# Seven block products for eight in the down projection and the embeddings' gate of a hybrid encoder

## The chip, the cores and the metric

The kernel runs on one core of one Trainium2 chip. The metric is the device time of one execution in microseconds (us). The engines are named as in the profile: PE is TensorE's matmul and PEld its weight load, DVE is VectorE, ACT is ScalarE, POOL is GpSimd and SP is SyncE, which here only issues DMAs.

## The reference

One layer of an encoder works on x of 2048 rows by 1024 columns, all in float32:

```python
h = layer_norm(x, emb_ln_g, emb_ln_b)
z = h @ w_in                                     # 1024 x 1536
y_ssm = s5_mixer(z[..., :512], ...)              # diagonal state space, GELU, GLU
y_sgu = sgu_mixer(z[..., 512:], ...)             # gated unit, blocks of 128 rows
mix = concatenate([rms_norm(y_ssm), rms_norm(y_sgu)]) @ w_out
h = layer_norm(ALPHA * h + mix, ln1_g, ln1_b)
ffn = (silu(h @ w_ffn_gate) * (h @ w_ffn_up)) @ w_ffn_down    # 1024 -> 2816 -> 1024
ple = (p @ w_ple) * sigmoid(h @ w_ple_gate + b_ple_gate)      # p: 2048 x 256
out = layer_norm(ALPHA * h + ffn + ple, ln2_g, ln2_b)
```

## The kernel before

A product in the precision that is wanted takes three passes: each operand is split into a rounded part `hi` (a copy on ACT, line 63) and the rest `lo` (a subtraction on DVE, line 64), and `mm3` (lines 68 to 70) adds hi·hi, hi·lo and lo·hi in one bank of PSUM. A pass is one matmul of a 128x128 stationary block against 512 columns. `load_w` (line 262) loads weights through SP into one of three `raw` tiles of 128x1024, and the split halves stand in six `wsp` tiles. PSUM is eight banks, all from `bank()`. Instructions are emitted in program order with a priority. A scheduler lays them out on each engine in advance, so an engine takes them in a fixed order and waits in it.

`run` has three parts. The first makes `z` and the gated unit. The second is the state space part: for every four of the 32 groups `s5_coeffs` makes coefficient matrices (`CA1`, `BA`, `yrep` and `dg` on POOL, `CA2` on DVE), `s5_matrices` turns them on PE, and for each group `s5_in` runs the scan on DVE (lines 803 to 811) and `s5_out` the output products. Then `glu` and `out_proj`. The third is `phase_b`: `mixed` finishes `out_proj`, normalizes, writes the rows to `xnd` and their transposes to `hfd` in device memory, and two blocks of 1024 rows go through the rest.

For a block, `heads` and `others` load the transposes and split them, `sums_B` makes on POOL the four sums of the right hand operand (lines 1219 to 1222), which Winograd's form of seven products needs, and `ple` does the embeddings: for each half of the rows and of the columns, 4 row tiles by 8 k by three passes with `w_ple_gate`, then the bias and the sigmoid (lines 1123 and 1124), `p @ w_ple`, and the product of both into `acc`. Then 11 rounds (`i`) follow, each with 256 of the 2816 inner columns: `gate` and `up` go through `quarters`, seven products of 4 k by three passes, with sums of the weights on POOL in `ops_A` (lines 1234 to 1241, tile `S`). `up` multiplies and splits the result into four `ff` tiles. `down` of the round before stands between them: for 16 tiles of 128x512, two k by three passes, and DVE adds each bank to `acc` (line 1319). `residual` adds ALPHA·h in four steps a round, on POOL, with `rx` tiles loaded from `xnd` (lines 1141 to 1150). At the block's end `norm_out` normalizes the eight `acc` tiles (line 135 and 136 on DVE, 1167 on ACT, 1168 and 1169 on POOL) and stores them.

Of the kernel before, what the change touches and what calls it, by code (L numbers as in the profile page):

```python
# [13 lines left out]
P = 128  # L14
S = 2048
# [7 lines left out]
FF = 2816  # L23
ALPHA = 2.0 ** 0.25
# [25 lines left out]
class Kern:  # L50
# [100 lines left out]
    def run(self):  # L151
        nc, tc = self.nc, self.tc
        with ExitStack() as ctx:
# [17 lines left out]
            self.xnd = dt([S, D], F32, name="xnd")  # L171
            with ExitStack() as c1:
# [530 lines left out]
    def s5_setup(self, ctx):  # L703
# [5 lines left out]
        nc.gpsimd.memset(self.yrep, 0.0)  # L709
        for i in range(2):  # L710
# [7 lines left out]
    def s5_coeffs(self, q):  # L718

        nc, pl = self.nc, self.pl  # L720
        v, g = nc.vector, nc.gpsimd
# [9 lines left out]
        ar8 = self.akr[:, gs, 1:9].unsqueeze(3).broadcast_to(sh8)  # L731
        ai8 = self.aki[:, gs, 1:9].unsqueeze(3).broadcast_to(sh8)
# [4 lines left out]
        g.tensor_tensor(out=ca, in0=X1.broadcast_to(sh9), in1=ar9, op=ALU.mult)  # L737
        g.tensor_tensor(out=tA, in0=X2.broadcast_to(sh9), in1=ai9, op=ALU.mult)
        g.tensor_tensor(out=ca, in0=ca, in1=tA, op=ALU.add)
        CA2 = pl.tile(sh8, F32, name="CA2", tag="CA2", bufs=2)  # L740
        tB = pl.tile(sh8, F32, name="tB", tag="tB", bufs=1)
        v.tensor_tensor(out=CA2, in0=X2.broadcast_to(sh8), in1=ar8, op=ALU.mult)
        v.tensor_tensor(out=tB, in0=X1.broadcast_to(sh8), in1=ai8, op=ALU.mult)
        v.tensor_tensor(out=CA2, in0=CA2, in1=tB, op=ALU.subtract)
        BA = pl.tile(sh8, F32, name="BA", tag="BA", bufs=1)
        tC = pl.tile(sh8, F32, name="tC", tag="tC", bufs=1)
        g.tensor_tensor(out=BA, in0=Y1.broadcast_to(sh8), in1=rr8, op=ALU.mult)
        g.tensor_tensor(out=tC, in0=Y2.broadcast_to(sh8), in1=ri8, op=ALU.mult)
        g.tensor_tensor(out=BA, in0=BA, in1=tC, op=ALU.add)
        shq = [P, NQ, L // 2, HG]  # L750
        for par in range(2):
            yv = yrep[:, :, par].rearrange("p g (s two) h -> p g s two h", two=2)
            g.tensor_copy(out=yv[:, :, :, par, :], in_=Y1.broadcast_to(shq))
        self.dg = pl.tile([P, NQ, P], F32, name="dg", tag="tC", bufs=1)
        g.tensor_tensor(out=self.dg, in0=self.ident.unsqueeze(1).broadcast_to([P, NQ, P]),
                        in1=self.dvec[:, gs].unsqueeze(2).broadcast_to([P, NQ, P]), op=ALU.mult)
        self.mats[q] = (T, CA1, CA2, BA)

    def s5_matrices(self, q):
        nc, pl = self.nc, self.pl  # L760
        v, yrep = nc.vector, self.yrep
        T, CA1, CA2, BA = self.mats[q]
# [200 lines left out]
    def phase_b(self, ctx):  # L963
# [6 lines left out]
        for _ in range(3):  # L970
            next(mixed)
        B = self.heads(0)
        next(mixed)
        for blk in range(2):
# [3 lines left out]
            if blk == 0:  # L978
                for _ in mixed:
                    pass  # L980
# [369 lines left out]
```

## Time and profile before

| | |
|---|---|
| time of three runs | 2375.39 to 2377.78 us, median 2377.55 us |
| the profiled execution's own time | 2384.52 us |
| its span, first to last instruction | 2382.5 us |
| its mean granted TensorE clock | 0.973 |
| matmuls | 9876 |
| moved by DMA | 257.27 MB, mean 108 GB/s |

The page gives busy time for each engine over the span. A matmul is recorded with 0.39 us, though the next one begins 0.227 us after it: they overlap, and a PE that is busy all the time need not be doing all it can. What a matmul costs is therefore read from the starts. Two windows matter besides the busy shares: the waits (who waited for whom) and the chain of work that ended last. In the second and third quarter of the span the same pattern repeats every 60.5 us, one round of the inner loop.

### The profile page before, as it was taken

Reading aid. Unit: us, or ns where it says so; the run is one execution under the profiler, and the core shown is the slowest. Engines: PE = TensorE matmul, PEld = TensorE weight load, DVE = VectorE, ACT = ScalarE, POOL = GpSimd, SP = SyncE. Lnnn points to the kernel's source line nnn. Section 1 sums busy time; section 2 is a strip of 40 time slices with the busy share of each in tenths; the row PEclk is TensorE's granted clock in tenths of the full one; section 3 lists DMA queues with packets and bytes.
Section 4 is the critical chain, followed back from the end, with each engine's and each line's share of the span. In section 5 each row is a group of like instructions: output and inputs, shape, how many; then the busy total and the mean of one; then the engine's idle time right before and its main releaser. Section 6 shows DMA issues by size and latency. Waiting matters only on the chain.

```text
span 2382.5 us, 27557 instructions
## 1 busy us (share of the span) xinstructions
PE 2228.3 (94%) x9876; PEld 1826.3 (77%) x9876; DVE 1551.4 (65%) x2726; ACT 761.5 (32%) x1291; POOL 794.7 (33%) x775
## 2 busy tenths in 40 slices
PE   7899987898999989999999999969899999999994
PEld 6678876676788878888887878758788888878883
DVE  7996769968645555555655555775556555555558
ACT  4444432243323432222222222323422222222221
POOL 1188145300000244444334342123344444443214
PEclk9999999899999999999999999979999999999997
DMA  8547434446654522212212121354122222221112
GB/s 268 140 151 230 133 102 135 133 116 235 233 208 166 171 84 62 65 56 66 62 58 70 57 64 54 124 181 160 49 62 67 62 67 63 65 64 57 50 40 88
DMA packets 248700, 257.27 MB, mean 108 GB/s; under 512 B 55106, under 2 KB 183154, under 8 KB 248564
## 3 DMA queue, kind: packets, MB, share of 16 engines
q1 hardware_dynamic: 219572, 230.33, 30.7%
q10 hardware_dynamic: 27904, 20.98, 2.8%
q0 software_dynamic: 1088, 4.21, 0.5%
q8 instruction: 77, 1.26, 0.2%
q14 instruction: 59, 0.48, 0.1%
HBM read 200.93 MB, written 54.54 MB: 107 GB/s over the span
## 4 chain that ended last, share of the span: by engine, by line
PE 53%; POOL 7%; DVE 6%; issue 3%; ACT 3%; DMA 2%; POOLq 0%; ACTq 0%; SPq 0%; DVEq 0%
PE ps L68 18%; PE ps L70 17%; PE ps L69 17%; POOL tx L1294 3%; DMA tx<-hfd 2%; ACT ff L63 1%; DVE wsp L64 1%; DVE t L1274 1%; ACT wsp L63 1%; DVE t L1277 1%; DVE tx L1294 1%; PE ps L142 1%; DVE t L1270 1%; DVE acc L136 1%; POOL rx L1148 0%
## 5 line engine op out<-in xcount | busy, mean ns | idle before, releaser
L63 ACT CAST wsp<-raw 128x512 fp32r<-128x512 f32 x448 | 275.5, 622 | 790.7 <-PE ps L70 716.8
L64 DVE TENSOR_TENSOR wsp<-raw,wsp 128x512 fp32r<-128x512 f32 x438 | 342.6, 788 | 252.9 <-ACT wsp L63 250.5
L1319 DVE TENSOR_TENSOR acc<-acc,ps 128x512 f32<-128x512 f32 x352 | 240.6, 685 | 144.2 <-PE ps L70 143.3
L68 PE MATMUL ps<-wsp,ff 128*128 128x512 f32 x768 | 299.7, 390 | 4.1 <-ACT ff L63 4.1
L70 PE MATMUL ps<-wsp,ff 128*128 128x512 f32 x768 | 299.6, 390 | 0.0
L69 PE MATMUL ps<-wsp,ff 128*128 128x512 f32 x768 | 299.5, 390 | 0.0
L68 PE MATMUL ps<-hT,wsp 128*128 128x512 f32 x744 | 290.4, 391 | 5.7 <-ACT hT L308 5.7
L69 PE MATMUL ps<-hT,wsp 128*128 128x512 f32 x744 | 290.4, 391 | 1.0 <-DVE hT L309 1.0
L70 PE MATMUL ps<-hT,wsp 128*128 128x512 f32 x744 | 289.9, 390 | 0.0
L68 PE MATMUL ps<-hTx,wsp 128*128 128x512 f32 x616 | 244.4, 397 | 25.0 <-DVE t L1123 13.4
L70 PE MATMUL ps<-hTx,wsp 128*128 128x512 f32 x616 | 241.3, 392 | 0.0
L69 PE MATMUL ps<-hTx,wsp 128*128 128x512 f32 x616 | 241.3, 392 | 0.0
L1234 POOL TENSOR_TENSOR S<-raw 128x512 f32<-128x512 f32 x44 | 58.7, 1333 | 438.3 <-DMA raw<-in_w_ffn_up_dram 318.4
L68 PEld LDWEIGHTS ps<-wsp,ff 128*128 128x128 f32 x768 | 144.4, 188 | 34.9 <-ACT ff L63 4.9
L70 PEld LDWEIGHTS ps<-wsp,ff 128*128 128x128 f32 x768 | 144.6, 188 | 30.5 <-DVE ff L64 0.5
L69 PEld LDWEIGHTS ps<-wsp,ff 128*128 128x128 f32 x768 | 144.6, 188 | 29.9
L68 PEld LDWEIGHTS ps<-hT,wsp 128*128 128x128 f32 x744 | 140.3, 189 | 34.9 <-ACT hT L308 6.1
L69 PEld LDWEIGHTS ps<-hT,wsp 128*128 128x128 f32 x744 | 140.0, 188 | 31.0 <-DVE hT L309 2.2
L70 PEld LDWEIGHTS ps<-hT,wsp 128*128 128x128 f32 x744 | 140.1, 188 | 29.1
L68 PEld LDWEIGHTS ps<-hTx,wsp 128*128 128x128 f32 x616 | 116.5, 189 | 58.7 <-ACT tx L1259 19.9
L64 DVE TENSOR_TENSOR ff<-tx,ff 128x512 fp32r<-128x512 f32 x96 | 67.1, 699 | 119.6 <-ACT ff L63 119.4
L69 PE MATMUL ps<-wsp,hT 128*128 128x512 f32 x352 | 138.6, 394 | 4.7 <-DVE wsp L64 4.7
(314 smaller groups left out, 4241.6 us busy)
## 6 DMA issues: line engine op xcount, KB each, us to landing
raw<-in_w_in_dram SPq DMA_DIRECT2D x48, 512.0 KB
raw<-in_w_ffn_gate_dram SPq DMA_DIRECT2D x44, 512.0 KB
raw<-in_w_ffn_up_dram SPq DMA_DIRECT2D x44, 512.0 KB
raw<-in_w_ffn_down_dram SPq DMA_DIRECT2D x44, 512.0 KB
tx<-hfd SPq DMA_DIRECT2D x64, 256.0 KB
raw<-in_w_ple_gate_dram SPq DMA_DIRECT2D x32, 512.0 KB
CS<-tbd SPq DMA_DIRECT2D x64, 128.5 KB
xt<-in_x_dram SPq DMA_DIRECT2D x16, 512.0 KB
```

What stands on the lines that cost most here:

```text
L63: nc.scalar.copy(out=hi, in_=src)
L64: (e or nc.vector).tensor_tensor(out=lo, in0=src, in1=hi.bitcast(F32), op=ALU.subtract)
L68: mm(ps, lhsT=lh, rhs=rh, start=start, stop=False, skip_group_check=more)
L69: mm(ps, lhsT=lh, rhs=rl, start=False, stop=False, skip_group_check=more)
L70: mm(ps, lhsT=ll, rhs=rh, start=False, stop=stop, skip_group_check=more)
L136: nc.vector.scalar_tensor_tensor(out=dst, in0=dst, scalar=rstd, in1=b, op0=ALU.mult, op1=ALU.add)
L142: self.nc.tensor.transpose(ps[:, t * P:(t + 1) * P], x[:, col:col + P], self.ident)
L1234: g.tensor_tensor(out=s1, in0=a21, in1=a22, op=ALU.add)
L1270: v.tensor_tensor(out=y, in0=y, in1=d, op=ALU.add)
L1274: v.tensor_tensor(out=z, in0=x, in1=c, op=ALU.add)
L1294: e.tensor_tensor(out=f[n], in0=f[n], in1=q, op=ALU.mult)
L1319: v.tensor_tensor(out=xs, in0=xs, in1=ps, op=ALU.add)
```

## The change

`down` leaves the rounds. `up` no longer splits its result: it multiplies all four quarters on DVE, makes the sums that the seven products need from the left operand (four on DVE), and stores seven tiles of 128x512 a round to device memory (`fod`), through ACT's queue. In the first block `down_sums` loads `w_ffn_down` in every round, makes four sums of it on POOL and stores them (`wtd`). After the 11 rounds the new `down` runs seven block products. Each goes over 11 steps: load a left and a right tile of 128x512 (256 KB each, two DMAs into one `raw` tile), split both, four row tiles by three passes. `seven` holds two sets of four banks, so that sums of products form in PSUM, and reads each set once a product (four additions on DVE a product, where 16 a round stood). `residual` runs beside products 0 to 3 with tiles of 128x512; the next block's operands and sums are made between the products (`operands(1)`); `norm_out` of a block's first half is issued after product 5, the rest between the products of the next block's `ple`. The last product of the last block loads all its operands first and then finishes one row tile after another.

`ple` does the gate for both halves of the rows as seven products of 4 k, with weight sums made on POOL in `gate_sums` during `mixed` and stored to `pgd`. The bias comes in by PE (a matmul of 33 rows, as `mixed` does), 12 for a block.

In the state space part `CA1` and `BA` move from POOL to DVE, `CA2` becomes one matmul of `CA1` with a signed permutation (float32, 512 columns, one for four groups) and a copy on ACT, `yrep` and `dg` move to ACT. `tx` gets six buffers for four.

```diff
+    def seven(self, product, read):
+        u = [self.bank() for _ in range(4)]
+        product(0, u, True)
+        read(0, u)
+        yield
+        for n in range(1, 7):
+            if n % 2:
+                if n < 5:
+                    q = [self.bank() for _ in range(4)]
+                product(n, q, n < 5)
+                read(n, q)
+            else:
+                product(n, u, False)
+                read(n, u)
+            yield
...
     def phase_b(self, ctx):
...
+            for i in range(NP):
+                f = self.gate(w_g, i, self.B)
+                if blk == 0:
+                    self.down_sums(i)
+                self.up(blk, w_u, i, self.B, f)
+            B = self.operands(1) if blk == 0 else iter(())
+            tail = self.norm_out(blk, accs)
+            for _ in self.down(blk, accs, tail):
+                next(B, None)
...
+    def gate_sums(self, kks):
...
+        for kk in kks:
+            rA, rB = (self.load_w(W[kk][:, :, i * 512:(i + 1) * 512], 1024) for i in range(2))
...
+            g.tensor_tensor(out=a22, in0=a21, in1=a22, op=ALU.add)
+            g.tensor_tensor(out=a21, in0=a11, in1=a21, op=ALU.subtract)
+            g.tensor_tensor(out=a11, in0=a22, in1=a11, op=ALU.subtract)
+            g.tensor_tensor(out=a12, in0=a12, in1=a11, op=ALU.subtract)
+            self.nc.sync.dma_start(out=self.pgd[kk, 0], in_=rA)
+            self.nc.sync.dma_start(out=self.pgd[kk, 1], in_=rB)
...
     def ple(...):
+        def product(n, ps, start):
+            src, b = ops[n]
+            for k in range(4):
+                if k % 2 == 0:
+                    w = self.load_split(src(k), 1024)
+                h = self.B[b][k]
...
+                for t in range(4):
+                    self.mm3(ps[t], h[:, 0, t * P:(t + 1) * P], h[:, 1, t * P:(t + 1) * P],
+                             w[:, 0, ws], w[:, 1, ws], start and k == 0, k == 3, not start)
...
     def residual(self, blk, accs):
+        for tg in range(2):
+            for hf in range(2):
...
+                gb = self.pb.tile([P, 2, 512], F32, name="S", tag="S", bufs=1)
...
                 for t in range(4):
+                    x = self.txt()
...
     def up(...):
-            e = nc.vector if n in (0, 3) else nc.gpsimd
-            e.tensor_tensor(out=f[n], in0=f[n], in1=q, op=ALU.mult)
-            h = self.fft()
-            self.split(h[:, 0], h[:, 1], f[n])
...
+            v.tensor_tensor(out=f[n], in0=f[n], in1=q, op=ALU.mult)
...
+        store(0, a11)
+        store(6, a22)
+        v.tensor_tensor(out=s1, in0=a21, in1=a22, op=ALU.add)
+        store(3, s1)
+        v.tensor_tensor(out=s2, in0=s1, in1=a11, op=ALU.subtract)
...
     def down(...):
-            for ii in range(2):
-                ft = fts[ii][tg]
-                self.mm3(ps, ft[:, 0, t * P:(t + 1) * P], ft[:, 1, t * P:(t + 1) * P],
-                         w[hf][ii][:, 0], w[hf][ii][:, 1], ii == 0, ii == 1)
-            xs = accs[tg][t][:, cs]
-            v.tensor_tensor(out=xs, in0=xs, in1=ps, op=ALU.add)
+        def operands(n, i, kept):
+            r = self.rawt()
+            nc.sync.dma_start(out=r[:, :512], in_=self.fod[blk, i, n])
+            nc.sync.dma_start(out=r[:, 512:], in_=w[n](i))
+            out = []
+            for ii in range(2):
+                if kept:
+                    t = self.hTt() if 2 * i + ii < 14 else self.hxt()
+                else:
+                    t = self.wspt() if ii else self.fft()
+                self.split(t[:, 0], t[:, 1], r[:, ii * 512:(ii + 1) * 512])
+                out.append(t)
+            return out
...
+        def product(n, ps, start):
+            if n == 6 and blk:
+                ops = [operands(n, i, True) for i in range(NP)]
+                for t in range(4):
+                    for i in range(NP):
+                        passes(ps, t, i, ops[i], start)
+                return
+            for i in range(NP):
+                ops = operands(n, i, False)
+                for t in range(4):
+                    passes(ps, t, i, ops, start)
...
+        for n, _ in enumerate(self.seven(product, read)):
+            if n < 4:
+                next(rest)
+            if n == 5:
+                next(tail)
+                next(tail)
+            yield
...
     def s5_matrices(self, q):
+        psC = self.bank()
+        nc.tensor.matmul(psC, lhsT=self.swap, rhs=CA1[:, :, 2:10, :].rearrange("p g s h -> p g (s h)"),
+                         start=True, stop=True)
+        CA2 = pl.tile([P, NQ, L, HG], F32, name="CA2", tag="CA2", bufs=2)
+        nc.scalar.copy(out=CA2.rearrange("p g s h -> p (g s h)"), in_=psC)
```

## Rows read from the trace of the kernel before

**Rows 1.** The page, part 1: busy us, share of the span, instructions.

```profile
PE 2228.3 (94%) x9876; PEld 1826.3 (77%) x9876; DVE 1551.4 (65%) x2726; ACT 761.5 (32%) x1291; POOL 794.7 (33%) x775
```

**Rows 2.** Stretch, inner loop: busy PE, PEld, DVE, ACT, POOL; clock, DMA share, GB/s.

```profile
1800.00:1860.00 60.00, 59.67 (x264) 49.06 (x263) 35.97 (x50) 16.27 (x28) 26.29 (x24) 1.00 0.20 63
```

**Rows 3.** Timeline of PE: start, us; `down`'s first matmul and the first behind it.

```profile
1801.45 0.39 PE L68 MATMUL ps<-wsp,ff 128*128 128x512 f32 x1
...
1823.21 0.39 PE L68 MATMUL ps<-hTx,wsp 128*128 128x512 f32 x1
```

**Rows 4.** The chain that ended last: start, us; one step of two successive rounds.

```profile
958.23 0.70 DVE t L1270
...
1018.72 0.70 DVE t L1270
```

**Rows 5.** The same chain, out_proj: four bias matmuls.

```profile
641.43 1.13 PE ps L1030 x4
```

**Rows 6.** Waits of PE, 1500 to 1700 us: total us, times, longest.

```profile
PE ps L69 <- DVE wsp L64: 23.4, 1, 23.4
PE ps L68 <- DVE t L1123: 6.4, 1, 6.4
```

**Rows 7.** Waits of PE, 640 to 870 us.

```profile
PE ps L68 <- DVE t L1123: 7.0, 1, 7.0
```

**Rows 8.** Stretches between the blocks and at the second loop's start, columns as rows 2.

```profile
1550.00:1560.00 10.00, 0.00 (x0) 0.00 (x0) 10.00 (x19) 1.02 (x1) 9.92 (x4) 0.50 0.26 104
...
1680.00:1690.00 10.00, 9.26 (x31) 7.52 (x32) 8.99 (x15) 7.12 (x13) 1.96 (x2) 0.71 0.21 59
```

**Rows 9.** Timeline of DVE, 1500 to 1560 us: `norm_out` between the blocks.

```profile
1552.84 2.87 DVE L136 SCALAR_TENSOR_TENSOR acc<-acc,rs,ff 128x1024 f32<-128x1024 f32 x1
```

**Rows 10.** Stretch at the end, columns as rows 2.

```profile
2350.00:2360.00 10.00, 1.86 (x9) 1.21 (x7) 9.96 (x42) 1.99 (x3) 9.84 (x5) 0.74 0.14 56
```

**Rows 11.** The chain that ended last: its last step.

```profile
2377.57 1.28 DVE acc L136
```

**Rows 12.** Stretch in the state space part, columns as rows 2.

```profile
400.00:420.00 20.00, 16.74 (x75) 13.21 (x74) 19.92 (x31) 6.78 (x15) 11.67 (x11) 0.84 0.53 165
```

**Rows 13.** Groups, 300 to 490 us: count, busy us, mean ns, idle before.

```profile
L811 DVE TENSOR_TENSOR PQ<-Sx,CS 128x512 f32<-128x512 f32 x32 | 30.8, 962 | 0.3
...
L739 POOL TENSOR_TENSOR ca<-ca,tA 128x576 f32<-128x576 f32 x7 | 11.1, 1590 | 0.5
```

**Rows 14.** Groups over the span: `glu`'s four products in plain float32.

```profile
L884 PE MATMUL ps<-vs,ones 128*128 128x512 f32 x8 | 4.1, 592 | 0.0
```

**Rows 15.** Timeline of DVE, inner loop: a split alone, one beside POOL.

```profile
1814.15 0.68 DVE L64 TENSOR_TENSOR wsp<-S,wsp 128x512 fp32r<-128x512 f32 x1
...
1829.51 1.63 DVE L64 TENSOR_TENSOR wsp<-raw,wsp 128x512 fp32r<-128x512 f32 x1 [1.32 <-ACT wsp L63]
```

**Rows 16.** Timeline of POOL, inner loop: a step of `residual`, a sum of `ops_A`.

```profile
1815.39 0.74 POOL L1147 TENSOR_TENSOR rx<-rx,rg 128x256 f32<-128x256 f32 x1
...
1829.31 1.29 POOL L1239 TENSOR_TENSOR raw<-raw 128x512 f32<-128x512 f32 x1
```

**Rows 17.** The page, part 5: groups of instructions on DVE.

```profile
L64 DVE TENSOR_TENSOR wsp<-raw,wsp 128x512 fp32r<-128x512 f32 x438 | 342.6, 788 | 252.9 <-ACT wsp L63 250.5
L1319 DVE TENSOR_TENSOR acc<-acc,ps 128x512 f32<-128x512 f32 x352 | 240.6, 685 | 144.2 <-PE ps L70 143.3
```

**Rows 18.** Timeline of SP, out_proj: four loads of `w_out`, 512 KB each.

```profile
590.30 8.99 SPq L262 DMA_DIRECT2D raw<-in_w_out_dram  x4
```

**Rows 19.** Timeline of ACT: casts of the first and the last of these four.

```profile
594.69 1.14 ACT L63 CAST hTx<-raw 128x512 fp32r<-128x512 f32 x2 [0.96 <-DMA raw<-in_w_out_dram]
...
602.70 1.15 ACT L63 CAST ff<-raw 128x512 fp32r<-128x512 f32 x2 [2.17 <-DMA raw<-in_w_out_dram]
```

**Rows 20.** Stretch around these loads, columns as rows 2.

```profile
580.00:600.00 20.00, 20.00 (x88) 16.01 (x87) 17.64 (x32) 7.26 (x13) 1.92 (x1) 1.00 0.69 219
```

More of the change, by code (lines that the diff above doesn't have):

```diff
@@ L23 @@
 FF = 2816
+NP = FF // (2 * P)
 ALPHA = 2.0 ** 0.25
@@ new lines, in down_sums @@
+    def down_sums(self, i):
+        g = self.nc.gpsimd
+        w_d = self.a["w_ffn_down"][0].rearrange("(k p) c -> p k c", p=P)
+        rA, rB = (self.load_w(w_d[:, 2 * i + ii, :], 1024) for ii in range(2))
+        b11, b12, b21, b22 = rA[:, :512], rA[:, 512:], rB[:, :512], rB[:, 512:]
+        g.tensor_tensor(out=b22, in0=b22, in1=b12, op=ALU.subtract)
+        g.tensor_tensor(out=b12, in0=b12, in1=b11, op=ALU.subtract)
+        g.tensor_tensor(out=b11, in0=b22, in1=b11, op=ALU.add)
+        g.tensor_tensor(out=b21, in0=b21, in1=b11, op=ALU.subtract)
+        self.nc.sync.dma_start(out=self.wtd[i, 0], in_=rA)
+        self.nc.sync.dma_start(out=self.wtd[i, 1], in_=rB)
@@ new lines, in bias, with sig @@
+        def bias(ps, half):
+            for t in range(4):
+                nc.tensor.matmul(ps[t], lhsT=one[0:33, :], rhs=rb[0:33, half, :], start=False, stop=True,
+                                 skip_group_check=True)
+        def sig(tg, hf, ps, add):
+            for t in range(4):
+                x = accs[tg][t][:, hf * 512:(hf + 1) * 512]
+                if add:
+                    v.tensor_tensor(out=x, in0=x, in1=ps[t], op=ALU.add)
+                nc.scalar.activation(out=x, in_=x if add else ps[t], func=AF.Sigmoid)
@@ L1150, in residual, with rows @@
                     g.tensor_tensor(out=xs, in0=xs, in1=x, op=ALU.add)
-                    yield
+                yield
+    def rows(self, src, scale):
+        nc = self.nc
+        rb = self.fft()
+        rbf = rb.rearrange("p a c -> p (a c)")
+        br = self.rawt()
+        nc.gpsimd.memset(rbf.bitcast(F32), 0.0)
+        for row in (0, 32):
+            nc.sync.dma_start(out=br[row:row + 1, :], in_=src.unsqueeze(0))
+            if scale != 1.0:
+                nc.scalar.mul(br[row:row + 1, :], br[row:row + 1, :], scale)
+            nc.scalar.copy(out=rbf[row:row + 1, :], in_=br[row:row + 1, :])
+        nc.vector.tensor_tensor(out=rbf[32:33, :], in0=br[32:33, :], in1=rbf[32:33, :].bitcast(F32),
+                                op=ALU.subtract)
+        return rb, self.one
@@ L1153, in norm_out @@
     def norm_out(self, blk, accs):
         nc, v, a = self.nc, self.nc.vector, self.a
[L1155 to L1171 removed]
+        last = blk == 1
```

311 lines of the change are left out of this document (167 added, 144 removed).

## The prediction

> **What bounds the kernel now.** I read the busy shares first. PE is busy 94% of the span and no other engine over 65% [rows 1]; in 60 us of the inner loop PE works 59.67 us, DVE 36, POOL 26, ACT 16, and DMA is at a fifth [rows 2]. Since matmuls overlap, the price of one comes from starts: `down`'s 96 matmuls of a round take from 1801.45 to 1823.21, so 21.76/96 = 0.2267 us each [rows 3]. A round is 60.49 us by two equal steps of the chain [rows 4], and its 264 matmuls (84 for `gate`, 84 for `up`, 96 for `down`) make 59.85; only 0.64 us a round is anything else. So in the loop time is the number of matmuls, and each that goes is worth 0.2267 us, as long as the other engines keep up with what replaces it.
>
> Outside the loop the waits of PE tell what is lost. Between the blocks PE stands still 23.4 us for a split that waits on DVE, and 6.4 us before the second loop [rows 6]; before the first loop it is 7.0 us [rows 7]. In the long gap PE does nothing while DVE and POOL are full [rows 8], both with `norm_out` [rows 9]. After each gap the clock is at its lower level for a while: in 1680 to 1690 it averages 0.71 and 31 matmuls start where 44 would. At the end PE stops near 2352 (1.86 us of the stretch from 2350) while DVE is full [rows 10], and DVE's last step ends at 2378.85 [rows 11]: a tail of some 30 us to the end of the span, again `norm_out`.
>
> **The change, part by part.** The sum is made against the profiled execution's own 2384.5 us, which lies 7.0 above the median of the three runs; I take 7 off at the end.
>
> Down projection: eight block products become seven. 2 blocks by 11 rounds by 96 = 2112 matmuls become 2 by 7 by 11 by 12 = 1848. 264 x 0.2267 = **-59.8**. The stationary and moving shapes stay, so the price of one does.
>
> Embeddings' gate: 768 become 672, 96 x 0.2267 = -21.8; the bias costs 24 matmuls of 33 rows, which go at 1.13 us for four [rows 5], +6.8. Together **-15.0**. DVE's bias additions (4 a half) become additions of partial sums; neutral.
>
> The seam between the blocks: `norm_out` is spread over the last product of `down` and the next `ple`, whose operands were split between the products before. The 23.4 and 6.4 us go, and about 5 us of low clock with them [rows 6, 8]. What is late next is the first weights of the second loop; I leave 5 us. **-30** (between -36, no gap, and -15, if the normalized tiles hold up `ple`'s third product, which writes into the same `acc` buffers). Before the first loop the gap of 7.0 came from sums made late on POOL; they are now needed already at `ple`'s third product, with two products (2 x 48 x 0.2267 = 22 us) as cover. **-6** (-10 to +10).
>
> The tail: of 30 us there remain the addition, statistics and scaling of one last tile, about 7 us by the steps in the trace, and the store, 3.7 us from DVE's end to the span's end [rows 11]. But the last product needs all of its 11 steps before its first row tile is done (33 matmuls, 7.5 us); loads at some 2.5 us a step keep it waiting perhaps 9 us. **-10** (-19 to 0).
>
> State space part: there DVE is the full engine, 19.92 of 20 us, PE has 3 us of room [rows 12]. For every four groups DVE gains six products and loses three, 3 x 0.68 = 2.1 us, 17 us in eight. But POOL falls silent there, and DVE's steps were stretched by it: `PQ` has a mean of 0.962 where one of its size takes 0.68 alone [rows 13, 15]. 32 of these give 9 us back, the scans and the small ones about as much. The new float32 matmul is 1.03 us (4.1 us for four calls) [rows 14], 8 in all, in PE's room. **-5** (-12 to +17).
>
> `up` and `gate` without `down` between them need 168 x 0.2267 = 38.1 us a round. DVE has there 14 splits, 10 additions, 4 products and 4 sums, 32 x 0.69 = 22 us; POOL 8 sums of `ops_A` and, in the first block, 4 of `down_sums`, 12 x 1.29 to 1.6 = 16 to 19 us [rows 16]. DVE no longer makes the 8 splits and 16 additions of `down` there. The weights' three `raw` tiles now hold six loads and two stores in 38 us, where they held six loads in 60. SP issues in order: behind a store of `wtd`, which waits for POOL, stands the load of `up`'s second tile. I count about 4 us of room, so **+5** (0 to +40). Seven stores a round on ACT's queue are 1.8 MB in 38 us, beside a DMA share of 0.2: nothing.
>
> `gate_sums` holds two of three `raw` tiles for four stretches in `out_proj`, which has room: **+2** (0 to +10).
>
> The new `down` is the open point, with no row of its own. A step is 12 matmuls, 2.72 us, and 77 a block. It needs 512 KB, 193 GB/s, two splits on ACT and DVE, and three `raw` tiles, so a tile must go round in 8.16 us. The nearest rows are `out_proj`'s weights: four loads of 512 KB [rows 18] are cast from 594.69 to 602.70, 2.67 us apart [rows 19], at a DMA share of 0.69 and 219 GB/s [rows 20]; they were also issued over 8.99 us, so free tiles set that spacing as much as DMA. So the supply is about as fast as PE, hardly faster; four steps are prepared ahead in `ff`, which hides jitter and no lasting lack.
>
> DVE is nearer to its limit. A product of 29.9 us has 22 splits (15.2 us alone) and 4 additions out of PSUM (2.7). Beside products 0 to 3 POOL has a quarter of `residual` each: 12 steps of 128x512, twice 0.74, and a scaling, some 19 us [rows 16]. A split that begins beside a POOL sum takes 1.63 us in place of 0.68: it waits for nearly the whole rest of that sum [rows 15, 16], and the mean of all 438 is 0.788 at POOL's one third [rows 17]. If the two add up, 15.2 + 19 = 34 us stand against 29.9, 4 us in each of eight products; the first block also has 28 splits and 16 sums for the next (19 + 21 us) and half of `norm_out` in product 6. Bounds: 0 (all of it finds gaps) to +60 (all of it adds up: 37 in products 0 to 3 of block one, 14 in block two's, 9 in the last ones). I take the two thirds that cannot move and little of the rest, since POOL's sums for the next block can slide into products 4 and 5: **+32**.
>
> The Trainium skill speaks against this part: "SBUF — State Buffer", section "Who interferes with whom", says that a VectorE instruction with two SBUF inputs and a GpSimd instruction that reads SBUF exclude one another for a whole instruction. The 1.63 us of the row agree. By that rule alone the term would be its upper end, +60.
>
> Sum: -59.8 - 15.0 - 30 - 6 - 10 - 5 + 5 + 2 + 32 = -86.8. 2384.5 - 86.8 = 2297.7, less 7: **2291 us**.
>
> **The rivals.** *PE keeps its pace in `down`.* For it: DVE has 30 us and PSUM reads fall from 16 to about 2.5 a round's worth. Against: the 1.63 us. Then the term is about 3 in place of 32: **2262**.
>
> *All of DVE's and POOL's work adds up, or the supply is a little slower than PE.* +60 in place of +32, or 3.1 us a step for 2.72 (154 x 0.38 = +59): **2320**. For it: rows 15, 18 to 20, and more transfers on the same queue (`xnd`, `hfd`). Against: `down` has spare time in products 4 to 6. The rule of the Trainium skill named above would end here.
>
> *Slower: the three `raw` tiles set the pace.* Where the two loads of a step stand in SP's order behind a load that waits for a POOL buffer, and the splits behind POOL, a round trip of 11.4 us in place of 8 makes a step 3.8 us: 154 x 1.08 = +166 in place of 32, **2425**. It decides from about 3.45 us a step (86.8 + 32 = 119 us over 154 steps is 0.77 above 2.72). For it: SP waits in order, and there is no fourth tile. Against: four loads in a row went 2.67 us apart beside other transfers.
>
> *The loop's weights come late in block one*, since six loads and two stores share three tiles: +40 in place of +5, **2326**. For it: the shorter round. Against: the 4 us of room counted above.
>
> **How the numbers follow.** The forecast, 2275 to 2305, has 0.42. PE's pace kept (2240 to 2275): 0.22. Work that adds up or supply a little slower (2305 to 2335): 0.20. Late weights: 0.06. The `raw` tiles as bound with a time over 2382: 0.06, and 0.04 for such a case that stops near the old time. From 2240 to 2335 there are some 0.86. A measurement here can tell 0.2%, 5 us, from no change: faster 0.91, the same 0.03, slower 0.06.
>
> **What would show it.** 336 fewer matmuls of three-pass work, and 32 new ones. Right: starts 0.227 us apart in `gate` and `up`, rounds of 38 to 39 us, no gap of 23 us between the blocks, a tail near 12 us. `down`'s seven products would take 209 us a block if PE keeps pace, 225 by the forecast, with PE waiting for `wsp` or `ff` on DVE, most in products 0 to 3 of the first block. Waits for DMA there would mean the supply. A state space part over 10 us longer would say that POOL's silence gave nothing back. Wrong would be a product of over 38 us on average.

## The result, and the profile after

The changed kernel takes 2449.58 us (median of four runs, 2446.67 to 2450.46) where the kernel before, on the same chip, takes 2377.66 (2375.39 to 2380.74): a ratio of 1.0299, with a 95% interval of 1.0282 to 1.0317. It is 72 us slower, where 87 us faster was forecast. The profiled execution spans 2447.0 us against 2382.5.

The page of the changed kernel, parts 1 and 2; columns as [rows 1].

```profile
PE 2216.9 (91%) x9556; PEld 1786.3 (73%) x9556; DVE 1582.4 (65%) x2672; ACT 870.7 (36%) x1495; POOL 761.2 (31%) x658
...
DMA packets 311147, 382.66 MB, mean 156 GB/s; under 512 B 61990, under 2 KB 179798, under 8 KB 311004
```

There are 320 matmuls fewer than in [rows 1], and POOL has less to do, not more. Beside PE no engine is busier than 65% of the span. So the time went into waiting, and the question is where. The starts of matmuls divide both spans into the same seven stretches:

| stretch | before, us | after, us | difference | forecast |
|---|---|---|---|---|
| up to the first transposes of `mixed` (state space part in it) | 612.1 | 588.2 | -23.9 | -5 |
| from there to the first `ple` (`gate_sums` in it) | 130.6 | 150.1 | +19.5 | +2 |
| first `ple`, up to the first round | 120.5 | 123.0 | +2.5 | -13.5 |
| block one: rounds and `down` | 674.4 | 772.9 | +98.5 | |
| block two: rounds and `down` | 670.8 | 684.5 | +13.7 | -13.8 with the line above |
| between the blocks, `ple` of block two in it | 143.1 | 108.7 | -34.4 | -37.5 |
| from the last matmul to the end | 31.0 | 19.6 | -11.4 | -19 |
| sum | 2382.5 | 2447.0 | +64.5 | -86.8 |

The forecast of -10 for the tail stands in two lines, as the prediction adds it up: -19 at the end, and +9 of waiting in the last product, which belongs to block two here. The two blocks hold 126 of the 151 us that separate the forecast from the result. Four stretches of 60 us in them, columns as [rows 2]: the rounds of block one, the rounds of block two, and in block two's `down` a stretch beside `residual` and one without.

```profile
1100.00:1160.00 60.00, 53.25 (x219) 42.72 (x218) 33.48 (x43) 17.71 (x30) 24.91 (x18) 0.94 0.35 110
1900.00:1960.00 60.00, 60.00 (x266) 49.69 (x265) 34.13 (x46) 20.25 (x34) 21.21 (x15) 1.00 0.30 95
2175.00:2235.00 60.00, 46.30 (x176) 34.94 (x175) 31.76 (x33) 16.39 (x29) 40.17 (x26) 0.89 0.55 181
2290.00:2350.00 60.00, 58.83 (x255) 47.08 (x254) 34.62 (x51) 23.99 (x42) 5.95 (x4) 1.00 0.57 186
```

The second line is what was forecast for all of the rounds: 266 matmuls in 60 us, the pace of [rows 3]. Block two's 1848 matmuls of `gate` and `up` take 419.3 us from first to last, 38.1 a round; block one's take 491.3, 44.7 a round. The last two lines show that the same `down` runs near PE's pace where POOL is nearly silent (255 matmuls) and at two thirds of it where POOL works (176), with DVE busy for only 32 of 60 us, ACT 16 and DMA 0.55. In all, `down` takes 277.3 us in block one and 260.7 in block two; at 0.2267 us a matmul it would be 209.5. Two things came as forecast: the pace and the seam. Waits of PE around the seam, as [rows 6]:

```profile
PE ps L69 <- ACT wsp L64: 5.0, 1, 5.0
PE ps L69 <- ACT ff L64: 3.1, 2, 2.1
PE ps L70 <- DVE wsp L65: 0.4, 1, 0.4
```

The 23.4 us are gone. Now the two places that lost. Block one's rounds (861.3 to 1352.6 us), first as a stretch, then SP's own waits in it:

```profile
861.30:1352.60 491.30, 444.29 (x1849) 358.76 (x1848) 279.13 (x348) 133.81 (x220) 196.48 (x133) 0.96 0.42 135
```

```profile
SPq L266 <- DVE wsp L65: 275.4, 39, 11.2
SPq L1112 <- POOL raw L1110: 87.1, 11, 8.1
SPq L266 <- DMA wtd<-raw: 27.1, 22, 2.1
```

SP waits for a `raw` tile to come free (line 266 is `load_w`): 275 us until DVE has split what lies in it, and 27 until the store of `wtd` has emptied it. At that store (line 1112) it waits 87 us for POOL's sums, 8 us in each of 11 rounds. Not all that PE loses is standing still. Behind most of its gaps of 3 to 5 us the granted clock is 0.50 for a while, and 82 matmuls of these rounds begin 0.43 us after the one before in place of 0.227: some 17 of the 72 us that these rounds take longer than block two's.

In block two's `down`, timeline of SP and then of POOL, 2184 to 2200 us:

```profile
2184.76 0.46 SPq L1444 DMA_DIRECT2D raw<-in_w_ffn_down_dram  x1
2198.49 0.33 SPq L1228 DMA_DIRECT2D tx<-xnd  x1
2198.93 0.37 SPq L1443 DMA_DIRECT2D raw<-fod  x1
```

```profile
2190.84 2.99 POOL L1229 TENSOR_TENSOR tx<-tx,S 128x512 f32<-128x512 f32 x2
2193.79 3.43 POOL L1230 TENSOR_TENSOR tx<-tx,S 128x512 f32<-128x512 f32 x2
2197.18 2.53 POOL L1232 TENSOR_TENSOR acc<-acc,tx 128x512 f32<-128x512 f32 x2
```

SP issues nothing for 13.3 us: it waits for a `tx` tile that POOL holds, for a load of `residual`, and the next operands of `down` (line 1443) stand behind it. PE runs on operands that were split ahead until 2199.3 us; then no matmul starts for 7.1 us. SP's waits in all of the first six products of block two's `down` (2166.7 to 2386.9 us; lines 1223 and 1228 load for `residual`):

```profile
SPq L1443 <- DVE ff L65: 97.3, 50, 4.2
SPq L1228 <- POOL acc L1232: 32.2, 6, 13.2
SPq L1223 <- POOL tx L1230: 10.6, 2, 8.6
```

And the splits beside POOL are long, as in [rows 15]. Groups in the same six products:

```profile
L65 DVE TENSOR_TENSOR ff<-raw,ff 128x512 fp32r<-128x512 f32 x66 | 59.1, 901 | 10.6 <-ACT ff L64 9.3 <-DMA tx<-xnd 1.3
L65 DVE TENSOR_TENSOR wsp<-raw,wsp 128x512 fp32r<-128x512 f32 x63 | 53.2, 848 | 84.5 <-ACT wsp L64 84.5
```

So three suspects stand in `down`: the **order** (SP behind POOL), the **port** (splits of 0.68 us that take up to 1.78 beside POOL) and the **ring** (three `raw` tiles in which the operands land). The experiments take them apart. Their measure is the time from the first to the last matmul of products 0 to 5 of block two's `down`: 792 matmuls, 179.6 us at PE's pace, 220.2 in the changed kernel. Block two is the cleaner place, for no operands of a next block are made there. The measure leaves out the gap between the last matmul of the rounds and the first of `down`, which is 4.4 us in the changed kernel and moves from run to run; it is given where that matters.

### The profile page after: what moved, and what is told of

Its sections match the earlier page's. It is cut to its first block, busy times and chain, and to the rows that moved or that the text cites. A ratio compares the mean times of both kernels' runs of the same rounds, so it can differ in the third digit from the quotient of the medians.

```text
span 2447.0 us, 27939 instructions
## 1 busy us (share of the span) xinstructions
PE 2216.9 (91%) x9556; PEld 1786.3 (73%) x9556; DVE 1582.4 (65%) x2672; ACT 870.7 (36%) x1495; POOL 761.2 (31%) x658
## 3 DMA queue, kind: packets, MB, share of 16 engines
q8 instruction: 75, 1.23, 0.2%
## 4 chain that ended last, share of the span: by engine, by line
PE 40%; DMA 20%; DVE 16%; issue 10%; POOL 10%; ACT 3%; SPq 1%; ACTq 0%; POOLq 0%; DVEq 0%
PE ps L70 12%; PE ps L69 12%; PE ps L71 12%; DMA raw<-wtd 4%; DMA raw<-in_w_ffn_up_dram 3%; DMA raw<-in_w_ffn_down_dram 3%; DVE wsp L65 2%; DVE ff L65 2%; DVE st L116 2%; ACT wsp L64 2%; DMA tx<-hfd 1%; DMA wtd<-raw 1%; POOL acc L1232 1%; POOL tx L1229 1%; POOL acc L1281 1%
## 5 line engine op out<-in xcount | busy, mean ns | idle before, releaser
L65 DVE TENSOR_TENSOR wsp<-raw,wsp 128x512 fp32r<-128x512 f32 x485 | 401.3, 833 | 416.0 <-ACT wsp L64 405.3
L64 ACT CAST wsp<-raw 128x512 fp32r<-128x512 f32 x495 | 304.6, 622 | 741.2 <-PE ps L71 326.6
L69 PE MATMUL ps<-wsp,ff 128*128 128x512 f32 x636 | 261.2, 411 | 43.7 <-ACT ff L64 34.1
L69 PE MATMUL ps<-hTx,wsp 128*128 128x512 f32 x616 | 250.2, 406 | 47.4 <-ACT tx L1373 26.9
L71 PE MATMUL ps<-wsp,ff 128*128 128x512 f32 x636 | 262.4, 414 | 31.1 <-DVE ff L65 31.0
L70 PE MATMUL ps<-wsp,ff 128*128 128x512 f32 x636 | 259.0, 407 | 4.6 <-DVE wsp L65 4.6
L70 PE MATMUL ps<-hTx,wsp 128*128 128x512 f32 x616 | 247.4, 402 | 0.0
L71 PE MATMUL ps<-hTx,wsp 128*128 128x512 f32 x616 | 246.9, 401 | 0.0
L69 PEld LDWEIGHTS ps<-wsp,ff 128*128 128x128 f32 x636 | 125.8, 198 | 77.4 <-ACT ff L64 41.8
L71 PEld LDWEIGHTS ps<-wsp,ff 128*128 128x128 f32 x636 | 125.9, 198 | 74.1 <-DVE ff L65 48.0
L64 ACT CAST wsp<-S 128x512 fp32r<-128x512 f32 x132 | 81.9, 621 | 275.3 <-PE ps L71 151.2
L70 PE MATMUL ps<-wsp,hT 128*128 128x512 f32 x400 | 157.3, 393 | 5.9 <-DVE wsp L65 5.9
L69 PE MATMUL ps<-wsp,hT 128*128 128x512 f32 x400 | 158.5, 396 | 1.3 <-DVE z L912 1.3
L71 PE MATMUL ps<-wsp,hT 128*128 128x512 f32 x400 | 157.2, 393 | 0.0
```

What stands on the lines that cost most here:

```text
L64: nc.scalar.copy(out=hi, in_=src)
L65: (e or nc.vector).tensor_tensor(out=lo, in0=src, in1=hi.bitcast(F32), op=ALU.subtract)
L69: mm(ps, lhsT=lh, rhs=rh, start=start, stop=False, skip_group_check=more)
L70: mm(ps, lhsT=lh, rhs=rl, start=False, stop=False, skip_group_check=more)
L71: mm(ps, lhsT=ll, rhs=rh, start=False, stop=stop, skip_group_check=more)
```

## The experiments

Experiments 1 to 3, 5 to 7 and 9 to 11 are one run each. Runs of one kernel lie up to 8 us apart here, so smaller differences of their totals say nothing. Stages repeat better: block two's rounds take 418.7 to 419.7 us in all runs but experiment 4, which has the old ones, and block two's first six products of `down` take 190.5, 190.5 and 190.8 in experiments 12 to 14, where they are the same.

### 1 to 3: each suspect alone

The kernel before was at 2379.3 us beside these runs.

**1. The residual's loads on POOL's queue**, so that SP never waits for them:

```diff
-                    nc.sync.dma_start(out=x, in_=self.xnd[r0:r0 + P, cs])
+                    g.dma_start(out=x, in_=self.xnd[r0:r0 + P, cs])
```

(and the same for the loads of the coefficients).

> The changed kernel with one edit: the loads of `residual` (rows of xnd, gain and bias) are issued from POOL's queue in place of SP's. POOL's arithmetic stays. Order theory (in `down` the operands' loads stand in SP's queue behind loads that wait for POOL to free a buffer): products 0 to 5 of the second block, 220 us in the changed kernel, fall to under 195, the first block's `down` from 277 to about 245, the whole from 2450 to about 2390. Port theory (POOL's sums hold up DVE's splits): POOL does the same work, so both stay within 8 us and the whole stays over 2435.

Measured: 2464.5 us, slower by 15. Products 0 to 5 take 218.8 us, block one's `down` 299.5. SP's waits for POOL are gone from block two's `down`; its wait for a free tile (line 1443, by DVE) grew from 97 us to 146. And single splits on DVE became very long. Timeline of DVE, then of POOL, in block one's `down`:

```profile
1417.16 10.40 DVE L65 TENSOR_TENSOR hTx<-tx,hTx 128x512 fp32r<-128x512 f32 x1
```

```profile
1416.61 0.55 POOL L1228 DMA_DIRECT2D tx<-xnd  x1
1417.19 1.30 POOL L1232 TENSOR_TENSOR acc<-acc,tx 128x512 f32<-128x512 f32 x1
1418.43 2.48 POOL L1229 TENSOR_TENSOR tx<-tx,S 128x512 f32<-128x512 f32 x2
```

This run removes one suspect and adds a cost of its own, so it says nothing against the order; experiment 10 does it cleanly.

**2. `down_sums` loads into `ff` tiles**, and leaves the three `raw` tiles to `gate` and `up`:

```diff
-        rA, rB = (self.load_w(w_d[:, 2 * i + ii, :], 1024) for ii in range(2))
+        rA, rB = (self.fft(F32).rearrange("p a c -> p (a c)") for _ in range(2))
+        for ii, r in enumerate((rA, rB)):
+            self.nc.sync.dma_start(out=r, in_=w_d[:, 2 * i + ii, :])
```

> The changed kernel with one edit: `down_sums` loads w_ffn_down into two `ff` tiles in place of two of the three `raw` tiles. The stores of the sums stay on SP. Ring theory (too few `raw` tiles for six loads and two stores in a round): the first block's loop, 491 us for 11 rounds, falls to 425 to 440, the whole to about 2390. Order theory (the load of `up`'s weights stands behind a store that waits for POOL): under 20 us of gain. Port theory: no gain.

Measured: 2390.8 us, 59 less. Block one's rounds, as a stretch and by SP's waits:

```profile
859.30:1285.40 426.10, 421.89 (x1848) 345.86 (x1847) 273.08 (x349) 133.43 (x220) 190.60 (x129) 1.00 0.46 153
```

```profile
SPq L266 <- DVE wsp L65: 223.2, 31, 11.0
SPq L1114 <- POOL ff L1112: 67.0, 10, 6.7
```

426.1 us in place of 491.3: 65 of the 72 us that block one's rounds had lost. SP still waits 67 us for POOL at the store, in front of `up`'s loads; what that order can cost is the 6.8 us by which these rounds are longer than block two's (419.3), and the shared tiles made the 65. The clock is back at 1.00 with it.

**3. The stores of `wtd` on POOL's queue** (changed kernel, `self.nc.sync` becomes `g` in the two stores of `down_sums`):

> The changed kernel with one edit: the two stores of `down_sums` are issued from POOL's queue in place of SP's; the `raw` tiles stay as they are. Order theory for the loop: the first block's loop falls from 491 to under 460 us, the whole to under 2420. Ring theory: `up`'s second load still waits until a stored tile is free, so the loop stays over 475 and the whole over 2430.

Measured: 2475.6 us, slower by 26, nearly all of it in block one's rounds (516.0 us). SP's waits in them:

```profile
SPq L266 <- DMA wtd<-raw: 160.9, 21, 13.0
```

SP is free of the store, and now waits 161 us for the `raw` tile that the store empties. With three shared tiles a freer order gains nothing.

### 4: the state space part alone

The kernel before with `s5_setup`, `s5_coeffs` and `s5_matrices` of the changed kernel.

> The kernel before with the change of the state space part alone (coefficients from POOL to DVE, one matmul and ACT copies for the rest). The forecast's theory (POOL's silence gives DVE more than the added products take): 5 to 10 us faster than before, 2368 to 2373. Rival (DVE, which was full, only gets more work): 5 to 17 us slower.

Measured: 2355.06 us, ratio 0.9903 (0.9878 to 0.9928): 24 us faster than the 2379.3 beside it (17 to 29 by the interval), where 5 to 10 were expected. The same stretch in the kernel before and in this one:

```profile
280.00:460.00 180.00, 154.25 (x706) 126.54 (x705) 152.46 (x273) 57.35 (x125) 85.67 (x77) 0.91 0.42 125
```

```profile
280.00:460.00 180.00, 168.44 (x825) 138.68 (x825) 149.48 (x327) 84.08 (x197) 2.23 (x6) 0.98 0.52 147
```

POOL falls from 86 to 2 us. DVE does 327 instructions where it did 273, in less time; `PQ` goes from 962 ns [rows 13] to

```profile
L817 DVE TENSOR_TENSOR PQ<-Sx,CS 128x512 f32<-128x512 f32 x32 | 21.9, 686 | 0.3
```

and PE gets 825 matmuls done for 706, at a granted clock of 0.98 for 0.91. The run doesn't say how much of the 24 is DVE's shorter steps, POOL's chain that is no longer waited for, or the clock.

### 5 to 8: arithmetic, ring, and both

From here on the base is the kernel of experiment 2 (2390.8 us), which leaves `down` as it was. The kernel before: 2383.3 us beside these four.

**5. The residual's arithmetic left out**, loads kept:

> The changed kernel with down_sums loading into ff tiles (the kernel of 2390.8 us), and in down the 48 POOL operations and the scaling of the residual left out for each block; its loads stay where they are in SP's order, so the residual is missing from the output. Port theory (POOL's arithmetic takes the splits on DVE from 0.68 to 1.75 us, and 2 x 1.75 us is more than the 2.72 us that PE needs for a step): both down stages fall from 280 and 266 us to 215 to 235, total 2285 to 2320. Order theory (loads of operands stand behind residual loads that wait for a tile held by POOL): the same fall, since nothing holds the tiles. Ring theory (three raw tiles, 8.2 us each at PE's pace, are too few for a load of 3 to 5 us, a cast, two splits and SP's queue): down stays at 260 to 280, total 2370 to 2390.

**6. Seven landing tiles** (three `raw`, four `ff`), split operands in `wsp` alone:

```diff
-            r = self.rawt()
+            r = self.rawt() if (n * NP + i) % 7 % 2 else self.fft(F32).rearrange("p a c -> p (a c)")
...
-                    t = self.wspt() if ii else self.fft()
+                    t = self.wspt()
```

> The kernel of 2390.8 us, with down's operands landing in seven tiles in turn (three raw, four ff) where there were three, and both split operands in wsp tiles; POOL's residual is kept. Ring theory: down falls to 215 to 235 us in each block, total 2290 to 2320. Port theory: DVE stays the limit wherever POOL is busy, down stays at 250 to 275, total 2360 to 2390. Order theory: loads run seven steps ahead, and a stop of 6 to 13 us in SP's queue is mostly covered, total 2300 to 2340.

**7. The residual on DVE**, one group of three operations in every third step of products 0 to 3, its load one group ahead:

```diff
-                    g.tensor_tensor(out=x, in0=x, in1=gb[:, 0], op=ALU.mult)
+            v.tensor_tensor(out=x, in0=x, in1=gb[:, 0], op=ALU.mult)
...
+                if n < 4 and i % 3 == 1:
+                    next(rest)
```

> The kernel of 2390.8 us, with the residual's 48 operations a block on DVE in place of POOL, one group of three in every third or fourth step of the first four products, its load one group ahead; raw is still three tiles. Port theory: the splits go back to 0.68 us, DVE has 98 us of splits and 33 us of residual in 210, down falls to 220 to 240 a block, total 2300 to 2340. Ring theory: down stays at 255 to 280, total 2370 to 2395. Order theory: as the port theory, since DVE frees the tiles at once.

**8. Both edits, 6 and 7:**

> Both edits together: seven landing tiles, residual on DVE. If either theory alone is whole, this is no better than the better one of the two single edits; if both causes are at work, down comes to PE's pace, 212 to 225 us a block, total 2270 to 2300, faster than before (2378).

Measured: 2339.4, 2361.1, 2342.2 and 2317.2 us; the last has a ratio of 0.9729 (0.9709 to 0.9748), which is slower than the 2270 to 2300 expected. Products 0 to 5 of block two, columns as [rows 2], in this order: the base, then the four.

```profile
2103.90:2328.90 225.00, 198.15 (x792) 153.49 (x793) 122.00 (x157) 75.71 (x133) 75.34 (x47) 0.93 0.55 181
```

```profile
2096.60:2277.80 181.20, 181.20 (x791) 149.86 (x792) 100.13 (x158) 76.10 (x133) 0.00 (x0) 0.99 0.62 198
```

```profile
2108.80:2307.80 199.00, 187.13 (x791) 151.36 (x792) 135.97 (x173) 85.47 (x151) 69.32 (x44) 0.96 0.65 214
```

```profile
2089.80:2280.10 190.30, 186.38 (x792) 150.82 (x793) 119.04 (x190) 76.73 (x134) 0.00 (x0) 0.98 0.63 203
```

```profile
2081.70:2263.80 182.10, 181.30 (x791) 149.60 (x792) 125.45 (x202) 85.52 (x151) 0.00 (x0) 0.99 0.70 224
```

Without POOL's arithmetic `down` runs at PE's pace with three tiles (181.2 against 179.6), with all loads of `residual` still on SP: the supply that the prediction doubted is enough. With the arithmetic and seven tiles it takes 199, on DVE 190, with both 182. The single edits save 26 and 35 us, together they would be 61 of an excess of 45: they work on the same loss. The gap ahead is 4.2 us in the base and 12.9, 10.8, 6.8 and 12.3 in the four; with it the products take 229.2, 194.1, 209.9, 197.0 and 194.4 us, so each edit is worth less than it looks, in the same order. The last product, without `residual`, is a case of the ring alone: 40.4 us from its first to its last matmul in the base, 39.9 without the arithmetic, 31.5 with seven tiles (29.7 at PE's pace). Block one's `down` goes from 280.4 to 256.9, 261.7, 261.5 and 236.0.

### 9 to 11: order and port taken apart

**9. The residual's arithmetic on POOL, without the loads of x:**

> The kernel of 2390.8 us, with the residual's 48 POOL operations a block and their places kept, and its loads left out: the first of each three reads the two coefficient rows in place of the loaded tile, so the residual in the output is not the reference's. Nothing of the residual stands in SP's order any more but the four loads of coefficients a block. Port theory: POOL runs its 48 operations back to back, the splits beside them stay at 1.2 to 1.8 us, and products 0 to 5 of block two stay at 205 to 230 us (225 with the loads, 181 with the loads and without the operations). Order theory: they fall to 181 to 195 us. Total 2365 to 2395 by the port, 2300 to 2340 by the order.

Measured: 2402.7 us, products 0 to 5 in 220.7 us. By the expectation that speaks against the order. But the trace shows that the run didn't remove the order. SP's waits there:

```profile
SPq L1225 <- POOL tx L1230: 28.8, 3, 13.9
```

Line 1225 loads the coefficients, into a single `S` tile that POOL reads to the end of a step, and `down`'s loads stand behind it. So the coefficients go too, but for one load at the start of each `down` (experiment 10), and then the same with seven landing tiles (experiment 11):

> The kernel of 2390.8 us, with the residual's 48 POOL operations a block kept in their places and all its loads but one left out: the two coefficient rows are loaded once for each down, nothing else, so SP never waits for POOL on the residual's account and the residual in the output is not the reference's. Order theory: SP waited some 42 us for POOL in block two's down; without these waits products 0 to 5 take 181 to 195 us (225 with all loads, 220.7 without the loads of x but with the four of coefficients, for which SP still waited 28.8 us). Port theory (the splits at 0.9 to 1.8 us, and three landing tiles that go round too slowly with them): 205 to 225 us. Total 2300 to 2340 by the order, 2365 to 2400 by the port.

> The same, with seven landing tiles for down (the kernel of 2361.1 us without the residual's loads). Here neither the order nor the number of tiles is left, so what products 0 to 5 take above 180 us is the port alone. By the port: POOL works 73 us on the residual, and in these DVE needs up to 2 x 1.75 us a step for 2.72: 190 to 200 us (199.1 with the loads). If the port costs PE nothing by itself: 180 to 186. Total 2345 to 2365 by the port, 2325 to 2340 without it.

Measured: 2370.6 and 2357.7 us. Products 0 to 5:

```profile
2107.30:2307.70 200.40, 190.28 (x791) 148.05 (x792) 133.21 (x157) 75.66 (x133) 74.04 (x44) 0.99 0.54 175
```

```profile
2115.00:2304.60 189.60, 184.17 (x791) 148.96 (x792) 147.80 (x174) 85.07 (x151) 70.95 (x41) 0.99 0.62 200
```

Neither theory wins. With three tiles the excess over 179.6 us is 45.4 in the base; the loads' order makes 24.6 of it (225.0 to 200.4), and what remains, 20.8, halves with seven tiles to 10.0. The loads took their transfers with them, but these alone cost nothing, for experiment 5 has them all and runs at PE's pace. With the gaps ahead (6.7 and 11.1 us) the two runs take 207.1 and 200.7: the order is worth 22 us, and in the second run 6 to 7 remain over experiments 5 and 8. So 6 to 10 us are left to the port, and a stretch of the second run shows its face, with one line of DVE's timeline in it:

```profile
2120.00:2180.00 60.00, 56.14 (x238) 43.66 (x237) 59.60 (x44) 22.83 (x40) 59.60 (x34) 1.00 0.54 171
```

```profile
2130.57 3.48 DVE L65 TENSOR_TENSOR wsp<-raw,wsp 128x512 fp32r<-128x512 f32 x2
```

DVE and POOL are both full. DVE's 44 instructions take 1.35 us on average (59.60/44), and where POOL's sums follow each other without a gap two splits take 3.48 us, more than PE's step of 2.72. DVE and POOL then alternate, one split and one sum every 1.70 us (2140.62 to 2144.03 us: two of each), where alone a split takes 0.69 and a sum 1.29. In block one neither run gains (285.3 and 269.8 us against 280.4 and 261.7): there the loads and sums for the next block stand in the same order, and no run separates them from the rest.

### 12 to 14: what else the new work beside POOL cost

**12. `gate_sums` one group later, landing tiles from `raw` on**, on the kernel of 2317.2 us (the kernel before: 2381.0 beside it):

```diff
-            self.gate_sums((tg, 3) if tg == 0 else (tg,))
+            self.gate_sums(((), (0, 1), (2, 3))[tg])
...
-            r = self.rawt() if (n * NP + i) % 7 % 2 else self.fft(F32).rearrange("p a c -> p (a c)")
+            r = self.rawt() if (n * NP + i) % 7 in (0, 2, 4) else self.fft(F32).rearrange("p a c -> p (a c)")
```

> The kernel of 2317.2 us with two moves: the sums of the embeddings' gate, of which two of four stood beside the first group of the mixed stage, are all made one group later (two and two beside the second and third group), and down's landing tiles begin with raw, since the ff tiles are still held by up's last sums. By the reading that the 8 loads and stores of the first two sums fill the DMA engines at 580 to 620 us (0.86 to 1.02 busy there): the first ff,hT product starts at 595 to 602 us where it started at 614, unless the later groups lose the same; the gap before each down falls from 12.4 to 4 to 9 us. Total 2285 to 2312; if both are hidden elsewhere, 2317.

Measured: 2305.39 us, ratio 0.9682 (0.9666 to 0.9698). The stretch of the first sums in the kernel of 2317.2 us, and here:

```profile
580.00:620.00 40.00, 27.83 (x117) 22.05 (x116) 17.60 (x23) 12.01 (x19) 5.72 (x4) 0.83 0.87 313
```

```profile
580.00:620.00 40.00, 39.51 (x187) 31.84 (x186) 19.88 (x33) 9.43 (x14) 5.16 (x4) 1.00 0.81 286
```

The first `ff`,`hT` product starts 17.5 us sooner, but the first `ple` only 7.2, the first round 3.9: the later groups lose most of it again. The gap of 12 us before each `down` is gone, and `down` takes 246 us for 236 and 190.5 for 182.1: most of it only moved.

**13. The layer norm of the last group ahead of the sums for block one** (two loops in `phase_b` exchanged; the kernel before: 2379.8):

> The kernel of 2305.4 us, with the layer norm and the transposes of the last group of the mixed stage put ahead of the sums and splits of block one's second operand group, which stood ahead of it on DVE and POOL. If the 7.1 us for which PE waits for DVE there (and the 6.5 us that PE stands idle beside it) come from those splits, which take 1.8 us each beside POOL: the first block's loop starts 4 to 10 us sooner, total 2295 to 2302. If the layer norm only moves the wait to the splits that the next product needs: total 2303 to 2312.

Measured: 2306.48 us, ratio 0.9686 (0.9669 to 0.9702), no change; the first product of `ple` takes 46.0 us where it took 23.5, and the first round starts 2 us later.

**14. `sums_B` on DVE** (`g` becomes `v` in its four operations), on the kernel of 2305.4 us:

> The kernel of 2305.4 us, with the 16 operations a block of sums_B on DVE in place of POOL. By the port: the splits beside them go from 1.8 to 0.69 us, DVE takes on 16 x 0.69 = 11 us and loses the waits of some 20 splits of 1.1 us each; block one's down falls from 246 us to 232 to 242, the first block's stage before its loop by 0 to 6 us, total 2288 to 2303. If the work on DVE counts and the port does not, DVE is fuller by 11 us where it is already 16 to 20 of 20: down 246 to 256, total 2305 to 2318.

Measured: 2279.67 us, ratio 0.9574 (0.9559 to 0.9589): 26 us less, below the 2288 to 2303 expected, and 100 us under the kernel before (2379.75 beside it). The same 60 us of block one's `down`, before and with this edit:

```profile
1340.00:1400.00 60.00, 52.33 (x204) 40.69 (x202) 49.97 (x73) 27.18 (x50) 22.17 (x16) 0.91 0.71 232
```

```profile
1340.00:1400.00 60.00, 58.22 (x250) 47.62 (x249) 56.81 (x94) 31.74 (x57) 0.00 (x0) 0.97 0.79 263
```

DVE takes 16 more operations a block (0.68 us each) and the program is shorter, 12.4 us before the first round and 12.7 in block one's `down`, by the starts of matmuls. `hT`'s splits in that `down` fall from a mean of 908 ns to 680. This is the fastest kernel of the study, and by 11 us faster than the forecast for the change.

## Why the prediction was wrong

**Rounds, "+5 (0 to +40)": +72.** This step failed by its own logic. It looked at SP's order ("behind a store of `wtd` ... stands the load of `up`'s second tile") and counted 4 us of room. Experiment 2 shows that the order cost at most 7 us and the count of tiles 65: six loads and two stores go round three tiles, and two of these stay with POOL's sums and the stores for a good part of each round (SP alone waits 8 us a round there). The rival "weights come late in block one" named the place and the three tiles, at a price of 40 and with a chance of 0.06.

**`down`'s DVE, POOL and supply, "+32 (0 to +60)": +119** (67.8 in block one, 51.2 in block two, of which 10.6 in the last product), and 9 us in the gaps before it; the kernel before lost 28.5 in its own rounds, which the sum had left in. This is the larger failure. The step added up busy times of DVE and POOL, 15.2 + 19 against 29.9 us a product. That is the port, and the port alone costs 6 to 10 us in block two (experiment 11), near the 14 named for its four products. What the sum left out is that the stretched work stands in two loops: a landing tile is free only after load, cast and two splits, and SP passes on no load while an earlier one waits for a tile of POOL's. Order makes 25 of 45 us in block two (22 of 35 over experiment 5, with the gap ahead), the ring with the port the rest. Block one's loss was not taken apart so far: its `down` is over 209.5 us by 71 in the kernel of 2390.8 us, 47 without the residual's arithmetic (experiment 5), 27 with both edits (experiment 8), and `sums_B` on DVE takes 13 off (experiment 14). The prediction's own sign of being wrong came, "a product of over 38 us on average": 538/14 is 38.4. The rival "slower" named both ("stand in SP's order behind a load that waits for a POOL buffer, and the splits behind POOL") and decided from 3.45 us a step: 538 us for 154 steps are 3.49. It had 0.06. Its "against" was the four loads of [rows 18], 2.67 us apart; those stood in a stretch where POOL worked 1.92 of 20 us [rows 20]. The row was measured with the suspect absent.

The Trainium skill's rule ("SBUF — State Buffer", section "Who interferes with whom": a VectorE instruction with two SBUF inputs and a GpSimd instruction that reads SBUF exclude one another) agrees nearly with the alternation above: a split and a sum together take 1.70 us there, and one after the other would take 1.98. Its price in the prediction, +60 from sums of busy time, was too low for `down` as a whole; in block two, with 14 of it, it was 4 to 8 us over what the port costs by itself, and in block one no run shows the port alone.

**State space part, "-5 (-12 to +17)": -24** by experiment 4. The signs were right and the size was not; POOL's silence gave back more than was counted, and no row of before had a price for it as a whole.

**`gate_sums`, "+2 (0 to +10)": +19.5.** "Which has room" had no row beside it. Timeline of ACT and SP in the changed kernel, where the first sums stand:

```profile
590.62 1.14 ACT L64 CAST hTx<-raw 128x512 fp32r<-128x512 f32 x2 [21.87 <-DMA raw<-in_w_out_dram]
592.07 0.34 SPq L1100 DMA_DIRECT2D pgd<-raw  x1
595.41 0.34 SPq L1099 DMA_DIRECT2D pgd<-raw  x1
595.86 4.70 SPq L266 DMA_DIRECT2D raw<-in_w_out_dram  x3
```

ACT is kept waiting 21.87 us for a load of `w_out`, and the next three loads stand in SP's order behind two stores of sums: the picture of `down` again. The sums also add 16 transfers of 512 KB, and the DMA engines are busy 0.87 of the time from 580 to 620 us; but the kernel before kept PE's pace beside a share of 0.86 (88 matmuls in the 20 us from 620). Which of tiles, order and transfers it was stays open. Moving the sums (experiment 12) gave 4 us in the end.

**First `ple`, -13.5: +2.5.** The fewer matmuls are there, but the layer norm of the last group waits on DVE behind splits beside POOL, which take 1.23 us on average for `hT`. Experiment 13 shows that its place doesn't matter, experiment 14 that taking the sums off POOL gives 12.4 us and brings these splits to 0.68.

**Tail, "-10 (-19 to 0)": -11.4** agrees by luck. The term was -19 at the end and +9 in the last product. The end gave 11.4 (19.6 us are left where the prediction says "near 12"), and the last product took 40.3 us from its first to its last matmul where PE's pace is 29.7, so both together gave about 1 us.

**Right:** 0.2267 us a matmul (-59.8 and the gate's), rounds of 38.1 us in block two, the seam (-34.4 for -37.5). The count of matmuls in the prediction's last paragraph, 336 fewer and 32 new, takes the bias in twice: 360 of three passes go and 24 come for the bias, and the state space part alone has 16 more records (9892 for 9876 in experiment 4), which makes the 320 of the page. For the two blocks the sum is then 72.5 (rounds) + 119 (`down`) + 8.6 (gaps before it) - 28.5 - 59.8 = 111.8, against 112.2 by the starts.

## What to carry to other kernels

Where matmuls are taken out, ask first how many tiles the operands land in, who holds each, and what stands in line behind a load that must wait; an average of busy times shows none of these: here PE lost 72 us in one loop and 119 in another while no other engine was busier than 65%. Price a supply only by rows in which the engines that will run beside it do run. That POOL is idle doesn't make work on it free: a split beside its sums takes up to 1.78 us for 0.68. Moving 48 operations a block of `residual` to a DVE that was busier saved 49 us with three tiles, where the order of its loads changed too, and moving 16 of `sums_B` saved 26.

## What the runs showed of the hardware

DVE and POOL side by side reached a state in which both were busy 59.60 of 60 us and DVE's operations took 1.35 us on average, about twice their time alone (experiment 11), while PE still did 238 of 265 matmuls. With loads issued from POOL's own queue between its sums, single splits took 10.40 and 10.85 us (experiment 1); in the changed kernel, where POOL issues no DMA in `down`, none took more than 1.82. The issue alone doesn't do it: in experiment 3 POOL issues 22 stores in block one's rounds, and no split takes more than 1.82 there either. What holds DVE in experiment 1 was not tried.
